# The order of the large products' matmuls: consecutive ones write different accumulators

## The chip, the core and the metric

The kernel runs on one core of one Trainium2 chip. The metric is the device time of one execution in microseconds, a median of three runs. TensorE (PE) multiplies, ScalarE (ACT) and VectorE (DVE) split the weights and evacuate the accumulators, SyncE (SP) starts the loads. Everything is computed in fp32 accuracy: each fp32 operand of a large product is split into a high and a low part of a matmul type ("hi" and "lo"), and hi·hi, hi·lo and lo·hi are summed.

## What is computed

Two transformer blocks run one after the other on 256 tokens of width 2048. What matters here are the products with weights; attention, convolution, pooling and norms lie between them.

```python
def first_block(x, ...):                      # two layers
    for l in range(DEPTH):
        h = _rms_norm(x, norm_g[l])
        proj = jnp.einsum('bsd,de->bse', h, w_in[l])           # 2048 -> 6208
        ...
        q_b = jnp.einsum('bsr,re->bse', _rms_norm(c_q, ...), w_uq[l])
        kv = jnp.einsum('bsr,re->bse', _rms_norm(c_kv, ...), w_ukv[l])
        ...
        x = x + jnp.einsum('bse,ed->bsd', mixed, w_out[l])     # 2048 -> 2048
    return _rms_norm(x, final_norm_g)

def second_block(x, mem, ...):                # one layer
    z = h @ w_in[l]                                            # 2048 -> 3584
    kv = m @ w_kv[l]
    ...
    x = x + mix @ w_out[l]
    u = causal_dwconv(h @ w_up[l], ffn_conv_w[l]) + ffn_conv_b[l]   # 2048 -> 11264
    gate, val = jnp.split(u, 2, axis=-1)
    x = x + (jax.nn.silu(gate) * val) @ w_down[l]              # 5632 -> 2048
    return rmsnorm(x, g_final)
```

## The kernel before

A large product takes 512 columns of a weight matrix at a time and sums over K in tiles of 128 rows ("k tiles"). `load_raw` (line 183) brings four k tiles of 512 columns in one transfer of 1 MB. `load_w` (line 188) splits them: ACT casts a k tile to `hi` (line 198), DVE subtracts and writes `lo` (line 199). Two k tiles make one hi tile and one lo tile; there are four buffers of each, so the split runs up to eight k tiles ahead of PE, and a cast into a buffer waits until PE has read the buffer's last user.

There are two kinds of product. `GemmA` gives tokens by columns: the activations are the stationary operand, the weights move. It has two accumulators, one for each half of the tokens, and three matmuls of up to 512 columns for each k tile and half (line 219). `GemmB` gives columns by tokens, in four blocks of 128 columns with one accumulator each: the weights are stationary and the activations move. For each k tile and block it has one matmul of 512 columns (hi weights times the hi and lo activations of all 256 tokens, line 244) and one of 256 columns (lo weights times hi activations, line 247).

One feed is two k tiles. Before, `GemmA.feed` goes through the halves in its outer loop, so six matmuls in a row write one accumulator; `GemmB.feed` goes through the blocks in its outer loop, so four in a row do.

The accumulators are PSUM banks. The pool `pg` (line 42) has four. A `GemmA` takes two of them, a `GemmB` all four, unless it is made with `alt=True`: then it takes the four banks of `pss`, `pst` and `pso`, which the attention and the transposes use as well. In the feed-forward part the products of the gate use `pg`, those of the value use the other four (lines 1040 and 1044). Elsewhere `GemmB` products follow one another, or are followed by a `GemmA`, in the same four banks of `pg`. A bank is free when its block has been evacuated: with a scale, ACT copies one half (line 256), DVE adds the other half out of PSUM (line 257) and multiplies (line 258). From line 257 on the next product may write the bank.

The products stand in the program one after another; `weave` puts pieces of attention between the feeds of a product. The order on each engine is then settled by a scheduler when the program is built, and each engine works through its instructions in that order.

Of the kernel before, what the change touches and what calls it, by code (L numbers as in the profile page):

```python
# [20 lines left out]
D = 2048  # L21
# [10 lines left out]
def net_kernel(ctx: ExitStack, tc: tile.TileContext, A: dict, out: bass.AP):  # L32
# [17 lines left out]
    def unit(shape, dt=F32, name="unit"):  # L50
        """A tile of 4 KiB per partition."""
        return units.tile(shape, dt, tag="u4", name=name)

# [1 line left out]
    xin = A["x"][0].rearrange("(t p) d -> p t d", p=128)  # L55
# [33 lines left out]
    cols = {}  # L89
# [28 lines left out]

# [1 line left out]
    def rsqrt(v, n, name):  # L120
# [47 lines left out]
    def bcast(col, name):  # L168
        """[128, 2] per-token column to [128, 256], the same on every partition."""
        dg = tp.tile([128, 2, 128], F32, tag="stage", name=f"{name}_d")  # L170
        for t in range(2):
            V.tensor_scalar(dg[:, t, :], ident, col[:, t:t + 1], None, ALU.mult)
        r = tp.tile([128, 256], F32, tag="R", name=name)

        def spread():
            p = pst.tile([128, 256], F32, tag="t", name=f"{name}_p")
            PE.matmul(p, ones, dg.rearrange("p t c -> p (t c)"), start=True, stop=True)
            V.tensor_copy(r, p)

        return r, spread  # L180

# [1 line left out]
    def load_raw(view, k0, nk, ncols):  # L183
# [19 lines left out]
    class GemmA:  # L203
        """out[tokens, cols], tokens in two tiles of 128; weights move."""

# [6 lines left out]
        def feed(self, items, act, tiles=(0, 1)):  # L212
            for t in tiles:
                for kt, hi, lo in items:
                    a = act(kt)
                    ah = a[:, 0, t * 128:(t + 1) * 128]
                    al = a[:, 1, t * 128:(t + 1) * 128]
                    for l, r in ((ah, hi), (al, hi), (ah, lo)):
                        PE.matmul(self.p[t][:, 0:self.w], l, r,  # L219
                                  start=self.c[t] == 0, stop=self.c[t] == self.n - 1)  # L220
                        self.c[t] += 1
# [4 lines left out]
    class GemmB:  # L226
        """out[cols, tokens] by blocks of 128 columns; tokens' hi and lo move."""

# [10 lines left out]
        def feed(self, items, act, bcols=None):  # L239
            for b in range(len(self.p)):  # L240
                for kt, hi, lo in items:
                    a = act(kt)
                    sl = slice(b * 128, (b + 1) * 128) if bcols is None else bcols(b)
                    PE.matmul(self.p[b], hi[:, sl], a.rearrange("p a t -> p (a t)"),  # L244
                              start=self.c[b] == 0, stop=False)
                    self.c[b] += 2
                    PE.matmul(self.p[b][:, 0:256], lo[:, sl], a[:, 0, :],  # L247
                              start=False, stop=self.c[b] == self.n)

# [10 lines left out]
    def gen(g, view, ncols, act, done=None, mid=()):  # L260
        """Feeds all of K; stops after each piece. mid: (first k after which, what to emit there)."""
        mid = dict(mid)
        for k0 in range(0, KT, 4):
            for it in load_w(view, k0, 4, ncols):
                g.feed(it, act)
                yield
            if k0 in mid:
                mid[k0]()
        if done:
            done(g)  # L270
# [6 lines left out]
    def weave(main, *fill, n=1):  # L277
        """One stage of main, then n pieces of fill, until both are through."""
        fill = itertools.chain(*fill)
        for _ in main:  # L280
            for _ in range(n):
                next(fill, None)
        run(fill)
# [11 lines left out]
    def lazy(make, *args, **kw):  # L295
        """A gen whose accumulators are taken when it starts."""
        yield from gen(make(), *args, **kw)
# [6 lines left out]
    def transpose_chunk(src, gcol, name):  # L304
        """src [128, 2, 512] token-major to [128, 4, hi/lo, 256] scaled by gcol[:, 0:4]."""
        dst = [unit([128, 2, 2, 256], F32R, f"{name}_{j}") for j in range(2)]
# [16 lines left out]

# [1 line left out]
    ssq = [cp.tile([128, 2, 4], F32, name=f"ssq{i}") for i in range(DEPTH + 3)]  # L325
# [36 lines left out]
    def setup_diff():  # L362
# [15 lines left out]

        # relative bias: r[h, i] for distance 255 - i, skewed through DRAM into T[p, h, c] = r[h, 127 - p + c]
        onehot = tp.tile([64, 384], F32, tag="pT", name="onehot", bufs=3)  # L380
# [76 lines left out]
    def bcast_row(row, name):  # L457
        """A row of D numbers on every partition."""
        ts_ = []
        for i in range(2):  # L460
            t = unit([128, 1024], F32, f"{name}{i}")
            SY.dma_start(t, row[i * 1024:(i + 1) * 1024].unsqueeze(0).to_broadcast([128, 1024]))
            ts_.append(t)
        return lambda n: ts_[n // 2][:, (n % 2) * 512:(n % 2 + 1) * 512]
# [25 lines left out]

# [1 line left out]
    rstd = keep(rstd0, 2, "rstd_0")  # L492
    HK = 0
    for l in range(DEPTH):
# [6 lines left out]

        # latent queries and keys, normalised and transposed; rotary key
        cT = []
# [34 lines left out]

        # second gate
        R, spread = bcast(rstd, f"R{l}")  # L540
# [81 lines left out]
        for i in range(2):  # L622
            SC.activation(sb[i], zb[i], AF.Silu)
        # latent attention, two heads at a time, among the products for the differential values
        M = [None] * 8
# [53 lines left out]

        # differential heads  # L680
        va = [unit([128, 2, 512], F32, f"va{i}") for i in range(2)]
# [79 lines left out]

        # output projection, residual, next hidden states
        wo = A["w_out"][l].rearrange("(k p) c -> p k c", p=128)
# [44 lines left out]

    # final norm of the first block, then the norm of the second one
    s2 = tp.tile([128, 2], F32, tag="ssq2", name="s2x")  # L810
# [6 lines left out]
    RX, spread = bcast(rx, "RX")  # L817
# [1 line left out]
    ivc = unit([128, 4, 256], F32, "ivc")  # L819
# [50 lines left out]
    def pool_out():  # L870
        yield
        yield
        # channels of group gi: even groups fill block b0 and the lower half of b1, odd ones the
        # upper half of b1 and block b2
        for blk in range(6):
# [18 lines left out]

    # queries and the attention over the memory
    g = runB(w[:, :, 3072:3584], 512, act, mid=[(HK, htail), (8, spread)])
# [44 lines left out]

    # pooling and convolution columns
    pol = [unit([128, 3, 256], F32, f"pooled{i}") for i in range(2)]
# [41 lines left out]

    # output projection and residual
    wo = A["w_out_2"][0].rearrange("(k p) c -> p k c", p=128)
# [29 lines left out]

# [1 line left out]
    act = tilesel(H)  # L1019
# [80 lines left out]
def _constants():  # L1100
    """Tables that depend on shapes alone."""
    f = np.float32
# [45 lines left out]
```

## Time and profile before

| | before |
|---|---|
| median of 3 runs | 1970.27 us (1970.2 to 1970.85) |
| span of the profiled execution | 1967.7 us |
| what lies around the span | 2.6 us |
| PE busy | 1952.5 us, 99% of the span |
| DVE busy | 1307.7 us, 66% |
| ACT busy | 1113.6 us, 57% |
| DMA | mean 191 GB/s |

The profile holds one execution, from its first instruction to its last: the span. The times of the runs are a little longer, as they hold the start and the end as well; the difference to the median is the third row. A matmul's row gives its start and its length; the length holds the time in which the result drains, which overlaps with the next matmul, so what one matmul costs is the distance from its start to the next start. Rows name tiles without their numbers: `gb` is any of a `GemmB`'s four accumulators in `pg`, `gbs`, `gbt` and `gbo` are those of a product with `alt=True`, `ga` is either half of a `GemmA`, `hf` the hidden states of the feed-forward part and `h` those of the layers.

### The profile page before, as it was taken

Reading aid. Unit: us, or ns where it says so; the run is one execution under the profiler, and the core shown is the slowest. Engines: PE = TensorE matmul, PEld = TensorE weight load, DVE = VectorE, ACT = ScalarE, POOL = GpSimd, SP = SyncE. Lnnn points to the kernel's source line nnn. Section 1 sums busy time; section 2 is a strip of 40 time slices with the busy share of each in tenths; the row PEclk is TensorE's granted clock in tenths of the full one; section 3 lists DMA queues with packets and bytes.
Section 4 is the critical chain, followed back from the end, with each engine's and each line's share of the span. In section 5 each row is a group of like instructions: output and inputs, shape, how many; then the busy total and the mean of one; then the engine's idle time right before and its main releaser. Section 6 shows DMA issues by size and latency. Waiting matters only on the chain.

```text
span 1967.7 us, 28785 instructions
## 1 busy us (share of the span) xinstructions
PE 1952.5 (99%) x10445; PEld 1665.0 (85%) x10445; DVE 1307.7 (66%) x2934; ACT 1113.6 (57%) x2403; POOL 10.1 (1%) x104
## 2 busy tenths in 40 slices
PE   8999999999999999999999999999999999999998
PEld 8988788888998788888887888888888888888887
DVE  6866556666576556766776676777786556777755
ACT  6755646665565555665554455665665445655544
POOL 0000000000000000000000000000000000000000
PEclk9999999999999999999999999999999999999999
DMA  8746455556665355456744566555556655555663
GB/s 253 274 161 195 153 177 166 172 171 227 197 202 183 122 168 167 158 193 222 250 151 153 180 229 231 176 195 207 193 177 209 225 203 182 176 190 202 217 222 129
DMA packets 190057, 376.66 MB, mean 191 GB/s; under 512 B 7495, under 2 KB 27994, under 8 KB 189786
## 3 DMA queue, kind: packets, MB, share of 16 engines
q1 hardware_dynamic: 189914, 374.82, 56.8%
q8 instruction: 82, 1.34, 0.3%
q14 instruction: 61, 0.50, 0.1%
HBM read 364.29 MB, written 12.07 MB: 191 GB/s over the span
## 4 chain that ended last, share of the span: by engine, by line
PE 98%; DVE 1%; ACT 1%; DMA 0%; issue 0%; ACTq 0%; SPq 0%; DVEq 0%
PE ga L219 40%; PE gb L244 23%; PE gb L247 12%; PE gbs L244 5%; PE gbs L247 2%; PE gbt L244 2%; PE gbo L244 2%; PE gbt L247 1%; PE gbo L247 1%; PE vb_ps L610 1%; PE s_b L640 1%; PE s_b L638 1%; PE s_a L708 1%; PE qr_ps L583 1%; PE pt L426 1%; PE pl_o L890 0%
## 5 line engine op out<-in xcount | busy, mean ns | idle before, releaser
L199 DVE TENSOR_TENSOR lo<-raw,hi 128x512 fp32r<-128x512 f32 (+4 forms) x1332 | 857.4, 679 | 532.6 <-ACT hi L198 527.6
L198 ACT CAST hi<-raw 128x512 fp32r<-128x512 f32 (+4 forms) x1332 | 756.3, 611 | 681.1 <-PE ga L219 260.9
L244 PE MATMUL gb<-h,hi 128*128 128x512 f32 x1088 | 389.0, 401 | 0.0
L247 PE MATMUL gb<-h,lo 128*128 128x256 f32 x1088 | 304.9, 280 | 0.0
L219 PE MATMUL ga<-hi,h 128*128 128x512 f32 (+2 forms) x896 | 261.0, 372 | 1.9 <-ACT hi L198 1.2
L244 PE MATMUL gb<-hf,hi 128*128 128x512 f32 x704 | 247.1, 396 | 0.0
L244 PEld LDWEIGHTS gb<-h,hi 128*128 128x128 f32 x1088 | 204.2, 188 | 49.5 <-issue 1.4
L219 PE MATMUL ga<-hi,gt 128*128 128x512 f32 (+1 forms) x784 | 221.0, 367 | 0.0
L247 PEld LDWEIGHTS gb<-h,lo 128*128 128x128 f32 x1088 | 205.3, 189 | 0.3
L247 PE MATMUL gb<-hf,lo 128*128 128x256 f32 x704 | 196.3, 279 | 0.0
L219 PEld LDWEIGHTS ga<-hi,h 128*128 128x128 f32 x896 | 160.7, 189 | 23.7 <-ACT hi L198 1.5
L219 PE MATMUL ga<-lo,h 128*128 128x512 f32 (+2 forms) x448 | 163.6, 366 | 0.0
L219 PEld LDWEIGHTS ga<-hi,gt 128*128 128x128 f32 x784 | 142.0, 189 | 24.4
L219 PE MATMUL ga<-hi,mix 128*128 128x512 f32 x512 | 161.1, 395 | 0.0
L244 PEld LDWEIGHTS gb<-hf,hi 128*128 128x128 f32 x704 | 132.1, 188 | 31.6
L219 PE MATMUL ga<-lo,gt 128*128 128x512 f32 (+1 forms) x392 | 144.0, 367 | 0.0
L247 PEld LDWEIGHTS gb<-hf,lo 128*128 128x128 f32 x704 | 132.6, 188 | 0.1
L244 PE MATMUL gbs<-hf,hi 128*128 128x512 f32 x352 | 127.1, 396 | 0.0
L219 PEld LDWEIGHTS ga<-hi,mix 128*128 128x128 f32 x512 | 94.5, 188 | 18.6
L219 PE MATMUL ga<-lo,mix 128*128 128x512 f32 x256 | 100.0, 391 | 0.0
L247 PE MATMUL gbs<-hf,lo 128*128 128x256 f32 x352 | 98.1, 279 | 0.0
L219 PEld LDWEIGHTS ga<-lo,h 128*128 128x128 f32 x448 | 84.3, 188 | 11.0
(336 smaller groups left out, 2575.2 us busy)
## 6 DMA issues: line engine op xcount, KB each, us to landing
raw<-in_w_in_dram SPq DMA_DIRECT2D x108, 1024.0 KB, 5.1
raw<-in_w_up_dram SPq DMA_DIRECT2D x88, 1024.0 KB, 4.9
raw<-in_w_out_dram SPq DMA_DIRECT2D x46, 1024.0 KB, 5.1
raw<-in_w_down_dram SPq DMA_DIRECT2D x39, 1024.0 KB, 5.2
raw<-in_w_in_dram SPq DMA_DIRECT2D x16, 704.0 KB, 4.3
raw<-in_w_kv_dram SPq DMA_DIRECT2D x8, 1024.0 KB, 5.3
raw<-in_w_ukv_dram SPq DMA_DIRECT2D x8, 1024.0 KB, 5.4
xdram<-x SPq DMA_DIRECT2D x16, 512.0 KB, 3.0
```

Of the source, the lines that this page charges most:

```text
L198: SC.copy(hi[:, i, :], raw[:, j + i, :])
L199: V.tensor_tensor(lo[:, i, :], raw[:, j + i, :], hi[:, i, :].bitcast(F32), ALU.subtract)
L219: PE.matmul(self.p[t][:, 0:self.w], l, r, start=self.c[t] == 0, stop=self.c[t] == self.n - 1)
L244: PE.matmul(self.p[b], hi[:, sl], a.rearrange("p a t -> p (a t)"), start=self.c[b] == 0, stop=False)
L247: PE.matmul(self.p[b][:, 0:256], lo[:, sl], a[:, 0, :], start=False, stop=self.c[b] == self.n)
L426: PE.transpose(pt[:, d:d + 128], e[:, j * 128:(j + 1) * 128], ident)
L583: PE.matmul(sp[:, t, 0:256], l_, r_.rearrange("p (h d) -> p h d", d=192)[:, :, 128:192], start=i == 0 and j == 0, stop=i == len(its) - 1 a ...
L610: PE.matmul(sp[:, t, :], l_, r_.rearrange("p (h d) -> p h d", d=256)[:, :, 128:256], start=n_[t] == 0, stop=n_[t] == 11)
L638: PE.matmul(s[:, a, c0:c1], qnT[hg][:, h % 4, q0:q0 + 128], knT[hg][:, h % 4, 0:kn], start=True, stop=False)
L640: PE.matmul(s[:, a, c0:c1], qrT[rs, hp, q0:q0 + 128], krT[rs, 0:kn], start=False, stop=True)
L708: PE.matmul(s[:, a, c0:c1], qa[rs, hh, q0:q0 + 128], ka[rs, hh, 0:kn], start=True, stop=True)
```

## The change

Both `feed` functions get another order of loops. In `GemmA` the halves are now the innermost loop: each of the three matmuls of a k tile is done for one half and then for the other. In `GemmB` the blocks are innermost: for each k tile first the four matmuls of 512 columns, one in each accumulator, then the four of 256 columns. The matmuls themselves, their operands, their number and the sums are the same. The changed lines stand at 217 (`ga`), 242 and 245 (`gb`) there. What else the diff holds are removed comments and docstrings, which move line numbers by two or three.

```diff
         def feed(self, items, act, tiles=(0, 1)):
-            for t in tiles:
-                for kt, hi, lo in items:
-                    a = act(kt)
-                    ah = a[:, 0, t * 128:(t + 1) * 128]
-                    al = a[:, 1, t * 128:(t + 1) * 128]
-                    for l, r in ((ah, hi), (al, hi), (ah, lo)):
-                        PE.matmul(self.p[t][:, 0:self.w], l, r,
+            for kt, hi, lo in items:
+                a = act(kt)
+                for h, r in ((0, hi), (1, hi), (0, lo)):
+                    for t in tiles:
+                        PE.matmul(self.p[t][:, 0:self.w], a[:, h, t * 128:(t + 1) * 128], r,
                                   start=self.c[t] == 0, stop=self.c[t] == self.n - 1)
                         self.c[t] += 1
...
         def feed(self, items, act, bcols=None):
-            for b in range(len(self.p)):
-                for kt, hi, lo in items:
-                    a = act(kt)
-                    sl = slice(b * 128, (b + 1) * 128) if bcols is None else bcols(b)
-                    PE.matmul(self.p[b], hi[:, sl], a.rearrange("p a t -> p (a t)"),
-                              start=self.c[b] == 0, stop=False)
+            for kt, hi, lo in items:
+                a = act(kt)
+                sl = [slice(b * 128, (b + 1) * 128) if bcols is None else bcols(b) for b in range(len(self.p))]
+                for b, p in enumerate(self.p):
+                    PE.matmul(p, hi[:, sl[b]], a.rearrange("p a t -> p (a t)"), start=self.c[b] == 0, stop=False)
                     self.c[b] += 2
-                    PE.matmul(self.p[b][:, 0:256], lo[:, sl], a[:, 0, :],
-                              start=False, stop=self.c[b] == self.n)
+                for b, p in enumerate(self.p):
+                    PE.matmul(p[:, 0:256], lo[:, sl[b]], a[:, 0, :], start=False, stop=self.c[b] == self.n)
```

How this stands on the engines is shown at one place, the end of the product for the first four query heads of the differential attention in the first layer (`gb0_2744` to `gb3_2747`, written to `qa0_2742`) and the start of the product for their keys (`gb0_2948` and on), which uses the same four banks. On PE, before, the last ten matmuls of the old product and the first two of the new one:

```order
L247 MATMUL gb1_2745<-h0_3_1_317,lo_2895 128x256
L244 MATMUL gb2_2746<-h0_3_1_317,hi_2894 128x512
L247 MATMUL gb2_2746<-h0_3_1_317,lo_2895 128x256
L244 MATMUL gb2_2746<-h0_3_1_317,hi_2894 128x512
L247 MATMUL gb2_2746<-h0_3_1_317,lo_2895 128x256
L244 MATMUL gb3_2747<-h0_3_1_317,hi_2894 128x512
L247 MATMUL gb3_2747<-h0_3_1_317,lo_2895 128x256
L244 MATMUL gb3_2747<-h0_3_1_317,hi_2894 128x512
L247 MATMUL gb3_2747<-h0_3_1_317,lo_2895 128x256
L244 MATMUL gb0_2948<-h0_0_0_118,hi_2954 128x512
L247 MATMUL gb0_2948<-h0_0_0_118,lo_2955 128x256
```

On PE now, the last eight of the old product and the first three of the new one:

```order
L242 MATMUL gb0_2744<-h0_3_1_317,hi_2894 128x512
L242 MATMUL gb1_2745<-h0_3_1_317,hi_2894 128x512
L242 MATMUL gb2_2746<-h0_3_1_317,hi_2894 128x512
L242 MATMUL gb3_2747<-h0_3_1_317,hi_2894 128x512
L245 MATMUL gb0_2744<-h0_3_1_317,lo_2895 128x256
L245 MATMUL gb1_2745<-h0_3_1_317,lo_2895 128x256
L245 MATMUL gb2_2746<-h0_3_1_317,lo_2895 128x256
L245 MATMUL gb3_2747<-h0_3_1_317,lo_2895 128x256
L242 MATMUL gb0_2948<-h0_0_0_118,hi_2954 128x512
L245 MATMUL gb0_2948<-h0_0_0_118,lo_2955 128x256
L242 MATMUL gb0_2948<-h0_0_0_118,hi_2954 128x512
```

The last matmul of the first accumulator stood twelve matmuls ahead of the old product's last one and stands three ahead of it now; the new product begins with that accumulator's bank, as before. On ACT the same place before (`hi_3006` is the hi tile of a later feed, in the buffer of `hi_2894`):

```order
L198 CAST hi_3000<-raw_2998 128x512 x2
L256 COPY ev_t_2932<-gb0_2744 128x256
L256 COPY ev_t_2936<-gb1_2745 128x256
L256 COPY ev_t_2940<-gb2_2746 128x256
L198 CAST hi_3006<-raw_2998 128x512
L256 COPY ev_t_2944<-gb3_2747 128x256
```

and now:

```order
L198 CAST hi_3000<-raw_2998 128x512 x2
L198 CAST hi_3006<-raw_2998 128x512
L253 COPY ev_t_2932<-gb0_2744 128x256
L253 COPY ev_t_2936<-gb1_2745 128x256
L253 COPY ev_t_2940<-gb2_2746 128x256
L253 COPY ev_t_2944<-gb3_2747 128x256
```

The first of the two casts to `hi_3006` has moved from behind the third evacuation to ahead of the first. On DVE the subtraction that belongs to it (`lo_3007`) has moved ahead of the additions; now it reads there:

```order
L199 TENSOR_TENSOR lo_3001<-raw_2998,hi_3000 128x512 x2
L199 TENSOR_TENSOR lo_3007<-raw_2998,hi_3006 128x512
L254 TENSOR_TENSOR ev_t_2932<-gb0_2744,ev_t_2932 128x256
L254 TENSOR_TENSOR ev_t_2936<-gb1_2745,ev_t_2936 128x256
L255 TENSOR_TENSOR qa0_2742<-ev_t_2932,R8_0_2212 128x256
```

Before, both halves of `lo_3007` stood behind all four evacuations.

## Rows read from the trace of the kernel before

**Rows 1.** The page: the span, the busy times of the engines with their number of instructions, and the chain that ended last by engine.

```profile
span 1967.7 us, 28785 instructions
...
PE 1952.5 (99%) x10445; PEld 1665.0 (85%) x10445; DVE 1307.7 (66%) x2934; ACT 1113.6 (57%) x2403; POOL 10.1 (1%) x104
...
PE 98%; DVE 1%; ACT 1%; DMA 0%; issue 0%; ACTq 0%; SPq 0%; DVEq 0%
```

**Rows 2.** Busy times in two stretches that cover nearly all of the span: start and end, length, busy us of each engine with its instructions, granted clock, DMA share, GB/s.

```profile
0.00:26.00 26.00, 20.36 (x107) 17.81 (x107) 15.66 (x47) 18.95 (x48) 0.38 (x7) 1.00 0.71 219
26.00:1960.00 1934.00, 1932.13 (x10338) 1647.23 (x10338) 1289.48 (x2878) 1093.34 (x2353) 9.71 (x97) 1.00 0.57 191
```

**Rows 3.** PE alone in order of time, in the output projection of the first layer, a `GemmA` with 512 columns: start us, length us, what, and how many in a row. The six matmuls from 476.23 write one half's accumulator, the six from 477.59 the other's, and from 478.95 it is the first one's again.

```profile
476.23 0.61 PE L219 MATMUL ga<-hi,mix 128*128 128x512 f32 x2
476.68 0.39 PE L219 MATMUL ga<-lo,mix 128*128 128x512 f32 x1
476.91 0.61 PE L219 MATMUL ga<-hi,mix 128*128 128x512 f32 x2
477.36 0.39 PE L219 MATMUL ga<-lo,mix 128*128 128x512 f32 x1
477.59 0.61 PE L219 MATMUL ga<-hi,mix 128*128 128x512 f32 x2
478.04 0.39 PE L219 MATMUL ga<-lo,mix 128*128 128x512 f32 x1
478.27 0.61 PE L219 MATMUL ga<-hi,mix 128*128 128x512 f32 x2
478.72 0.39 PE L219 MATMUL ga<-lo,mix 128*128 128x512 f32 x1
478.95 0.61 PE L219 MATMUL ga<-hi,mix 128*128 128x512 f32 x2
```

**Rows 4.** The same view near the end, in the only `GemmA` with 256 columns.

```profile
1935.00 0.40 PE L219 MATMUL ga<-hi,gt 128*128 128x256 f32 x2
1935.24 0.28 PE L219 MATMUL ga<-lo,gt 128*128 128x256 f32 x1
...
1936.08 0.40 PE L219 MATMUL ga<-hi,gt 128*128 128x256 f32 x2
```

**Rows 5.** The same view in the feed-forward part, a `GemmB`; eight pairs lie between the first and the last of these rows.

```profile
1301.30 0.39 PE L244 MATMUL gbt<-hf,hi 128*128 128x512 f32 x1
1301.53 0.27 PE L247 MATMUL gbt<-hf,lo 128*128 128x256 f32 x1
1301.64 0.40 PE L244 MATMUL gbt<-hf,hi 128*128 128x512 f32 x1
...
1304.07 0.39 PE L244 MATMUL gbt<-hf,hi 128*128 128x512 f32 x1
```

**Rows 6.** The same view at the place whose order is shown above: the last feed of the query product (eight pairs from 286.44) and the start of the key product at 289.27. The first accumulator's last matmul is the one at 287.04.

```profile
286.44 0.40 PE L244 MATMUL gb<-h,hi 128*128 128x512 f32 x1
286.68 0.28 PE L247 MATMUL gb<-h,lo 128*128 128x256 f32 x1
286.80 0.40 PE L244 MATMUL gb<-h,hi 128*128 128x512 f32 x1
287.04 0.28 PE L247 MATMUL gb<-h,lo 128*128 128x256 f32 x1
...
289.16 0.28 PE L247 MATMUL gb<-h,lo 128*128 128x256 f32 x1
289.27 0.40 PE L244 MATMUL gb<-h,hi 128*128 128x512 f32 x1
```

**Rows 7.** Two lines of the kernel with all their matmuls, by the tiles they read, the first and the last of each kind: count, then length in ns (least, median, greatest), first and last start. The eleven rows of line 244 hold 2,816 matmuls (704, 352, 176 and 176 of them read `hf`), line 247 as many; the ten of line 219 hold 3,768.

```profile
L244 PE MATMUL gb<-h,hi x1088: 389/395/582, 62.6 to 1111.1; 128*128 128x512 f32 x182
...
L244 PE MATMUL gbt<-h,hi x32: 392/394/395, 1068.4 to 1132.5; 128*128 128x512 f32 x32
```

```profile
L219 PE MATMUL ga<-hi,h x896: 318/389/690, 6.5 to 865.6; 128*128 128x512 f32 x103, 128*128 128x352 f32 x51, 128*128 128x384 f32 x26
...
L219 PE MATMUL ga<-lo,mixb x128: 387/389/397, 1134.0 to 1223.4; 128*128 128x512 f32 x128
```

**Rows 8.** ACT alone in order of time at the place of rows 6; in brackets the idle time ahead and what ended it.

```profile
286.52 1.14 ACT L198 CAST hi<-raw 128x512 fp32r<-128x512 f32 x2 [1.68 <-PE gb L244]
287.57 0.87 ACT L256 COPY ev_t<-gb 128x256 f32<-128x256 f32 x2
288.76 0.37 ACT L256 COPY ev_t<-gb 128x256 f32<-128x256 f32 x1 [0.32 <-PE gb L247]
289.36 0.62 ACT L198 CAST hi<-raw 128x512 fp32r<-128x512 f32 x1 [0.22 <-PE gb L244]
289.89 0.36 ACT L256 COPY ev_t<-gb 128x256 f32<-128x256 f32 x1
```

**Rows 9.** DVE alone at the same place.

```profile
287.18 1.29 DVE L199 TENSOR_TENSOR lo<-raw,hi 128x512 fp32r<-128x512 f32 x2 [1.53 <-ACT hi L198]
288.39 0.75 DVE L257 TENSOR_TENSOR ev_t<-gb,ev_t 128x256 f32<-128x256 f32 x2
```

**Rows 10.** All engines in order of time at a place where PE did wait for a bank: the fourth accumulator of a later query product, released by the addition on DVE.

```profile
343.35 0.42 DVE L257 TENSOR_TENSOR ev_t<-gb,ev_t 128x256 f32<-128x256 f32 x1
343.44 0.39 PE L435 MATMUL o_a<-va,pT 128*128 128x128 f32 x2
...
343.83 0.50 PE L244 MATMUL gb<-h,hi 128*128 128x512 f32 x1
...
344.16 0.28 PE L247 MATMUL gb<-h,lo 128*128 128x256 f32 x1
```

**Rows 11.** Who waited for whom: the waiting engine, tile and line, the one waited for, us in total, times, longest us.

```profile
ACT hi L198 <- PE ga L219: 260.9, 193, 4.0
...
ACT hi L198 <- PE gb L244: 194.3, 163, 2.5
```

## The prediction

> **What bounds the kernel now.** I read the page first: PE is busy for 99% of the span and makes 98% of the chain that ended last [rows 1]. Then the busy times by stretch: from 26 us on PE is busy for 1932.13 of 1934.00 us at a granted clock of 1.00, so it neither waits nor runs at the lower of its two clock levels [rows 2]. Only two things can therefore move the time: the step from one matmul's start to the next, and gaps in PE's work that are not there today. I read the steps from PE's own order of time in each kind of product, and the gaps from the three engines at one place where a product hands its accumulators to the next.
>
> **The step in the A products: no change.** In rows of 512 columns three matmuls take 0.68 us, 0.227 each [rows 3]. The accumulator changes between 477.36 and 477.59 and again between 478.72 and 478.95: 0.23 us both times, and the step from 476.68 to 476.91, where it does not change, is 0.23 as well. The 3,768 matmuls of line 219 [rows 7] already contain both cases at one price, so I cost the new order at 0. A row of 512 columns at 2.4 GHz streams for 0.213, so 0.013 us of each step is something else; the 256-column rows say the same (nine in 1.08 us, 0.120 each, against 0.107 of streaming [rows 4]).
>
> **The step in the B products: -6 us.** Here the trace has only alternating pairs of 512 and 256 columns. Eight pairs take 2.77 us in the feed-forward part, 0.346 a pair [rows 5], and 2.83 us, 0.354 a pair, at the query product [rows 6]. Four pairs, the work of one k tile, are 1.385 and 1.415. After the change a k tile is four matmuls of 512 and four of 256. By the nearest rows, those of the A products with equal neighbours, that is 3 x 0.227 + 3 x 0.120, and one alternating pair where the widths meet: 1.041 + 0.346 = 1.387, or 1.041 + 0.354 = 1.395. There are 2,816 pairs, 704 k tiles; half of the pairs read `hf` [rows 7]. So 352 x 0.002 = +1 and 352 x -0.020 = -7: I take -6. The bounds: every 512 as slow as the slowest here, 0.24 (286.44 to 286.68), gives 3 x 0.24 + 0.360 + 0.350 = 1.430 against a mean of 1.400, +21 us; every 256 as fast as 0.11 (1301.53 to 1301.64 [rows 5]) gives 0.681 + 0.330 + 0.350 = 1.361, -27 us. Both suppose that a step seen singly becomes the rule; I lean on the equal-neighbour rows and keep -12 to +8.
>
> The step of 0.120 is where I looked for a rule against the change: four matmuls of 256 columns in a row each need a new stationary operand of 128 columns. The Trainium skill, TensorE: Matmul & The Clock Gate, section LDWEIGHTS, gives such a load as columns over 1.2 GHz, 107 ns, as long as 256 columns stream, so by the page a run of 256s has nothing to spare, while in a pair the 512 has. The rows of the 256-column product agree with that (0.120 with a new operand each time), and the sum above already uses them; a load that took longer would cost 2,112 steps times the excess.
>
> **The gaps: +21 us.** This is the part that the loops don't show. A B product takes all four `pg` banks; a bank is free when DVE's addition (line 257) is through. Before, the first accumulator's last matmul starts at 287.04, 2.12 us ahead of the product's last one at 289.16 [rows 6]; its copy starts at 287.57 [rows 8], the first of two additions at 288.39, and half of the 0.75 later, at 288.77, the bank is free [rows 9]. PE asks for it at 289.27, half a microsecond later: no wait. From the last matmul's start to the free bank are 288.77 - 287.04 = 1.73 us. After the change the four accumulators end together: that matmul stands three ahead of the end, 3 x 0.120 = 0.36 us. With the old 1.73 the bank is free 1.37 us after the last matmul's start; PE could go on after 0.12. A gap of 1.25.
>
> The order adds to it. Ahead of the copies ACT now has a cast that waits for PE's last hi read; DVE has the subtraction of that cast ahead of the additions. Call T the start of the product's last matmul. The last 512 starts at T - 0.59 and its row is 0.40 long, so the cast starts at about T - 0.17. It takes 0.62 [rows 8], to T + 0.45; the copy starts within 0.53 of the cast (289.36 to 289.89) and is through at T + 0.73; the subtraction starts at T + 0.47, holds DVE for 0.60 (two and the first addition from 287.18 to 288.39 [rows 9]), so the addition runs from T + 1.07 to T + 1.47. Where PE did wait for a bank, its matmul started at 343.83, 0.06 after the addition's end at 343.77, and the next followed after 0.33 in place of 0.235, 0.10 more [rows 10]. So T + 1.53 against T + 0.12, and 0.10: **1.5 us** for one place.
>
> The places, from the code: query to key, key to second query, key to the second gate's A product, in two layers (6); memory keys to memory values (1); memory queries to the first columns, and the fifth to the first (2): 9 where nothing else stands between, 13.5 us. Seven have transposes, scores or values between, which PE can do meanwhile: the two gate products in each layer, the last gate to memory keys, second query to second key in each layer, sixth columns to fifth: half, 0.8 each, 5.5 us. The eight small products of w_uq and w_ukv have other matmuls beside them; 0.25 each, 2 us. The feed-forward part alternates two sets of banks and A products alternate pairs of banks: there the evacuation has a whole product's time, 0. The sum is 21; from 15 (the seven and the eight covered, 1.5 of slack lost) to 26 (all sixteen in full).
>
> **The sum.** 1967.7 + 21 - 6 = 1982.7 for the span; with the 2.6 that lie around it 1985.3, which compares to the median of 1970.27. I predict **1985 us**, 0.8% slower. Its own range is 1970.3 + 15 - 12 = 1973 to 1970.3 + 26 + 8 = 2004; I draw it a little closer, 1973 to 2000, as both ends at once are unlikely.
>
> **Rivals.**
> 1. The 0.013 us that each step has beyond streaming is the price of adding to the bank just written, and goes when neighbours write different banks. Over 3,768 + 5,632 matmuls that is 122 us, and with the gaps 1970 - 122 + 21 = 1869. Against it: the steps at which the accumulator changes cost the same to a hundredth [rows 3], in an A product and at every fourth matmul of a B product. 3%. The same skill page, section on the missing nanoseconds of a 56 ns step, puts back-to-back 512-column matmuls at 215.7 ns once warm, 11 ns below the 227 of this kernel; so by the page something here does cost extra, and that would be worth about 103 us if the order were its cause. The rows speak against that cause.
> 2. The B step gains more than I think, and the gaps are filled: the 512s behind one another fall to 0.227 and the 256s to 0.113 as the fast half of a pair in the query product does, 3 x 0.227 + 3 x 0.113 + 0.35 = 1.37 against 1.40, -21 us, and with only the nine bare places at 1.25 paid, +11: 1960. It decides for faster only if the gaps stay under 21. For it: casts wait for PE often (260.9 and 194.3 us [rows 11]), so the helpers are ahead. Against it: no row of 256 after 256 is below 0.12. 7%.
> 3. The gaps are hidden: the new product's operands have long been split, and if the additions ran ahead of the subtraction, only half the gap would be left at the bare places and none elsewhere, 9 x 0.7 = 6; with -6 from the step, 1970: no change. Against it: the order on ACT and DVE is fixed, and the cast and the subtraction stand ahead. 8%.
> 4. The evacuations, four at once in place of one every 0.7 us, starve the split. Then each of the 22 feed-forward products would lose about 1 us more: 2007. The casts' waits for PE [rows 11] say that the split is ahead by eight k tiles, 11 us; four evacuations take less. 6%.
>
> My forecast has 76%. Faster by over 0.2% (less than about 1966.3; 0.2% is what this kernel's runs can tell from nothing): rival 1, most of 2, 9%. Within 0.2%: rival 3 and the low tail, 10%. Slower: 81%.
>
> **What would show it.** The order of time at 289 us: PE idle for about 1.5 us with the addition on DVE as its releaser, and the same at the other eight bare places; PE's busy time nearly the same and the gaps listed under the B line's weight loads or matmuls as 15 to 25 us behind DVE's addition. The A steps stay at 0.227. In the feed-forward part no gap, and a k tile at 1.38 to 1.40. The prediction is wrong if A steps fall below 0.22, if 256 after 256 is not 0.120, or if PE goes on at a hand-over without a gap.

## The result: 1.25% slower, and the profile after

The changed kernel takes 1995.08 us (median of 4 runs, 1994.13 to 1995.5), the kernel before, on the same chip, 1970.56: the ratio is 1.0125, 95% interval 1.011 to 1.0139. Forecast were 1985 us. The page of the changed kernel, its lines of totals, its chain by engine, and two of its groups (line, engine, operation, count | busy us, mean ns of one | idle time just before them in us, and what ended it):

```profile
span 1993.7 us, 28835 instructions
...
PE 1960.8 (98%) x10445; PEld 1670.5 (84%) x10445; DVE 1303.6 (65%) x2934; ACT 1109.7 (56%) x2403; POOL 10.2 (1%) x104
...
PE 95%; DVE 2%; ACT 1%; DMA 1%; issue 0%; ACTq 0%; SPq 0%; DVEq 0%
...
L242 PE MATMUL gb<-h,hi 128*128 128x512 f32 x1088 | 309.8, 400 | 10.6 <-DVE ev_t L254 9.4
...
L242 PEld LDWEIGHTS gb<-h,hi 128*128 128x128 f32 x1088 | 185.5, 189 | 41.0 <-DVE ev_t L254 11.9
```

Against [rows 1] the span is 26.0 us longer. PE's idle time, span less busy time, goes from 15.2 to 32.9 us, +17.7; its busy time rises by 8.3. The other engines do the same work as before. On the chain PE falls by 3 points, and DVE and the DMAs stand one higher each: the end now hangs on other engines at times. The group names where: the first product line of the layers waits for line 254, DVE's addition that frees a bank. The list of who waited for whom says the same (us in total, times, longest us):

```profile
PEld gb L242 <- DVE ev_t L254: 13.0, 12, 1.5
...
PE gb L242 <- DVE ev_t L254: 9.8, 9, 1.3
...
PEld ga L217 <- DVE ev_t L254: 4.5, 3, 1.5
```

The loads (`PEld`) wait 13.0 us for it ahead of B products and 4.5 ahead of A products, 17.5 in all. The count of 9 in the second line is not that of the nine bare places: three of those stand ahead of an A product.

In the kernel before, the same wait is 0.4 us:

```profile
PEld gb L244 <- DVE ev_t L257: 0.4, 2, 0.2
```

Busy times by stretch, as in [rows 2], from 26 us to near the end:

```profile
26.00:1986.00 1960.00, 1940.30 (x10339) 1651.85 (x10338) 1285.84 (x2881) 1089.45 (x2353) 9.80 (x97) 1.00 0.57 188
```

The granted clock is 1.00 as before; PE lacks 19.7 us there where it lacked 1.9. So the loss is not the clock's: for most of it PE stands still.

One hand-over, the place of [rows 6, 8, 9]; the old product's last matmul now starts at 294.85 in place of 289.16. PE alone (start us, length us, what, how many in a row, in brackets the idle time ahead and what ended it):

```profile
292.16 1.09 PE L242 MATMUL gb<-h,hi 128*128 128x512 f32 x4
293.09 0.64 PE L245 MATMUL gb<-h,lo 128*128 128x256 f32 x4
293.57 1.09 PE L242 MATMUL gb<-h,hi 128*128 128x512 f32 x4
294.50 0.63 PE L245 MATMUL gb<-h,lo 128*128 128x256 f32 x4
296.43 0.50 PE L242 MATMUL gb<-h,hi 128*128 128x512 f32 x1 [1.30 <-DVE ev_t L254]
296.77 0.28 PE L245 MATMUL gb<-h,lo 128*128 128x256 f32 x1
```

ACT and then DVE at the same place:

```profile
294.70 0.62 ACT L198 CAST hi<-raw 128x512 fp32r<-128x512 f32 x1 [1.66 <-PE gb L242]
295.22 1.19 ACT L253 COPY ev_t<-gb 128x256 f32<-128x256 f32 x4
296.28 0.65 ACT L198 CAST hi<-raw 128x512 fp32r<-128x512 f32 x1
```

```profile
295.35 0.69 DVE L199 TENSOR_TENSOR lo<-raw,hi 128x512 fp32r<-128x512 f32 x1 [1.51 <-ACT hi L198]
295.96 0.74 DVE L254 TENSOR_TENSOR ev_t<-gb,ev_t 128x256 f32<-128x256 f32 x2
296.63 0.75 DVE L255 TENSOR_TENSOR qa<-ev_t,R 128x256 f32<-128x256 f32 x2
```

The old product's last matmul is the fourth from 294.50, three steps of 0.118 later: T = 294.85. The reader can follow the prediction's chain with it: cast at T - 0.15 (forecast -0.17), subtraction at T + 0.50 (0.47), addition at T + 1.11 (1.07) and 0.41 long, so through at T + 1.52 (1.47), PE at T + 1.58 (1.53), the next matmul 0.34 after it (0.33). Without the wait PE would have gone on at T + 0.12: 1.46 us are lost, and the late next matmul costs 0.10 more. All nine places that the prediction called bare show the wait, each between 1.45 and 1.46 us.

The steps, read from starts. An A product (six matmuls from 500.44 to 501.80, 0.227 each, as in [rows 3]) and a B product of the feed-forward part:

```profile
500.44 0.62 PE L217 MATMUL ga<-lo,mix 128*128 128x512 f32 x2
500.90 1.07 PE L217 MATMUL ga<-hi,mix 128*128 128x512 f32 x4
501.80 0.62 PE L217 MATMUL ga<-lo,mix 128*128 128x512 f32 x2
```

```profile
1298.42 1.09 PE L242 MATMUL gb<-hf,hi 128*128 128x512 f32 x4
1299.35 0.64 PE L245 MATMUL gb<-hf,lo 128*128 128x256 f32 x4
1299.83 1.09 PE L242 MATMUL gb<-hf,hi 128*128 128x512 f32 x4
1300.76 0.63 PE L245 MATMUL gb<-hf,lo 128*128 128x256 f32 x4
1301.23 1.09 PE L242 MATMUL gb<-hf,hi 128*128 128x512 f32 x4
```

A k tile of the B product takes 1.41 and 1.40 us here, against 1.385 in [rows 5]. Split by neighbours over the first group of feed-forward products, 512 after 512 steps by 0.2335 us on average, 512 to 256 by 0.2286, 256 to 256 by 0.1186, 256 to 512 by 0.1183; 3 x 0.2335 + 0.2286 + 3 x 0.1186 + 0.1183 = 1.403. No product of this part has a gap.

### The profile page after: what moved, and what is told of

It is laid out like the page before. It is cut to its first block, busy times and chain, and to the rows that moved or that the text cites. A ratio compares the mean times of both kernels' runs of the same rounds, so it can differ in the third digit from the quotient of the medians.

```text
span 1993.7 us, 28835 instructions
## 1 busy us (share of the span) xinstructions
PE 1960.8 (98%) x10445; PEld 1670.5 (84%) x10445; DVE 1303.6 (65%) x2934; ACT 1109.7 (56%) x2403; POOL 10.2 (1%) x104
## 4 chain that ended last, share of the span: by engine, by line
PE 95%; DVE 2%; ACT 1%; DMA 1%; issue 0%; ACTq 0%; SPq 0%; DVEq 0%
PE ga L217 38%; PE gb L242 23%; PE gb L245 11%; PE gbs L242 5%; PE gbs L245 2%; PE gbt L242 2%; PE gbo L242 2%; PE gbo L245 1%; PE gbt L245 1%; PE vb_ps L607 1%; DVE lo L199 1%; PE s_b L637 1%; PE s_b L635 1%; DMA raw<-in_w_in_dram 1%; ACT hi L198 1%; PE s_a L705 1%
## 5 line engine op out<-in xcount | busy, mean ns | idle before, releaser
L242 PE MATMUL gb<-h,hi 128*128 128x512 f32 x1088 | 309.8, 400 | 10.6 <-DVE ev_t L254 9.4
L217 PE MATMUL ga<-hi,h 128*128 128x512 f32 (+2 forms) x896 | 226.1, 373 | 4.7 <-DVE ev_t L254 2.6
L217 PE MATMUL ga<-hi,gt 128*128 128x512 f32 (+1 forms) x784 | 193.5, 367 | 0.0
L242 PE MATMUL gb<-hf,hi 128*128 128x512 f32 x704 | 193.0, 395 | 0.0
L245 PEld LDWEIGHTS gb<-h,lo 128*128 128x128 f32 x1088 | 169.9, 188 | 23.6
L245 PE MATMUL gb<-h,lo 128*128 128x256 f32 x1088 | 180.6, 281 | 0.0
L217 PE MATMUL ga<-lo,h 128*128 128x512 f32 (+2 forms) x448 | 127.6, 365 | 0.0
L217 PE MATMUL ga<-lo,gt 128*128 128x512 f32 (+1 forms) x392 | 114.1, 367 | 0.0
L245 PE MATMUL gb<-hf,lo 128*128 128x256 f32 x704 | 112.6, 281 | 0.0
L217 PEld LDWEIGHTS ga<-lo,gt 128*128 128x128 f32 x392 | 71.9, 189 | 12.2
```

Of the source, the lines that this page charges most:

```text
L217: PE.matmul(self.p[t][:, 0:self.w], a[:, h, t * 128:(t + 1) * 128], r, start=self.c[t] == 0, stop=self.c[t] == self.n - 1)
L242: PE.matmul(p, hi[:, sl[b]], a.rearrange("p a t -> p (a t)"), start=self.c[b] == 0, stop=False)
L245: PE.matmul(p[:, 0:256], lo[:, sl[b]], a[:, 0, :], start=False, stop=self.c[b] == self.n)
```

## The experiments

The theory to be tried (hand-over): rotating through the accumulators lets all four end together, their evacuation can no longer run beside the product's tail, and PE waits at each product that takes the same banks. Its rival (pace): the steps themselves became longer.

**The two halves of the change apart.** `e1_only_a` has the new order in `GemmA` alone, `e2_only_b` in `GemmB` alone (each a part of the diff above).

> Only the A products get the new order; the B products keep the old one. Theory 'hand-over' (the 24.5 us come from the four accumulators of a B product ending together, so that PE waits for a bank at the next product): A products alternate pairs of banks and no B product ends differently, so 1970 to 1971, the A steps at 0.227 us and no gap over 0.5 us after 30 us. Rival 'pace' (writing another accumulator at each step costs something everywhere): about a third of the loss, 1977 to 1980. My sum had 0 for this part.

Measured: 1971.93 us, ratio 1.0006 (0.9997 to 1.0015). The new order of the A products cannot be told from none.

> Only the B products get the new order; the A products keep the old one. Hand-over: the whole loss, 1993 to 1996, with nine gaps of about 1.45 us behind DVE's addition. Pace: two thirds of the loss, 1985 to 1988.

Measured: 1994.2 us, ratio 1.0119 (1.0104 to 1.0134). The loss is in the B products.

**Gaps or steps.** Two kernels exchange the order of one piece, the last two k tiles of each B product, against that of the rest. `e3_last_by_block` is the changed kernel with the last piece in the old order:

```diff
+            if self.c[0] + 2 * len(items) == self.n:
+                for b in range(len(self.p)):
+                    for kt, hi, lo in items:
+                        (the two matmuls of before)
+            else:
                 for kt, hi, lo in items:
                     (the eight matmuls of after)
```

`e4_last_rotating` is the kernel before with the last piece alone in the new order.

> As the changed kernel, but the last feed of each B product goes block by block as before, so that the four accumulators end one after another; 7 of 8 feeds keep the new order. Hand-over: the nine gaps vanish and 20 us or more come back, 1970 to 1974; what is left over 1970 is the price of the new steps. Pace: seven eighths of the loss stay, 1991 to 1993. A third theory, 'supply' (four evacuations at once delay the split of the weights): the evacuations are spread again here, so it expects 1970 to 1974 too, and differs from hand-over only in what PE waits for: hi and lo in place of the addition.

Measured: 1975.62 us, ratio 1.0025 (1.0016 to 1.0035). 19.5 us are back.

> The mirror of it: the kernel before, in which only the last feed of each B product rotates through the accumulators. Hand-over: nearly the whole loss, 1990 to 1994, with the same nine gaps. Pace: one eighth of the loss in the B products, 1972 to 1974.

Measured: 1988.87 us, ratio 1.0092 (1.0075 to 1.0108): 18.1 of the 24.5 us come with one piece of each product in the new order. Both kernels land on the hand-over's side of the two theories, and neither inside its range: the first is 1.6 us above, the second 1.1 below. PE at the same hand-over, first in `e3_last_by_block`, then in `e4_last_rotating`:

```profile
291.55 0.39 PE L243 MATMUL gb<-h,hi 128*128 128x512 f32 x1
291.78 0.28 PE L246 MATMUL gb<-h,lo 128*128 128x256 f32 x1
291.89 0.63 PE L253 MATMUL gb<-h,hi 128*128 128x512 f32 x2
```

```profile
292.13 0.63 PE L248 MATMUL gb<-h,lo 128*128 128x256 f32 x4
294.06 0.50 PE L254 MATMUL gb<-h,hi 128*128 128x512 f32 x1 [1.30 <-DVE ev_t L267]
```

In the first, the new product starts 0.11 us after the old one's last matmul; in the second, the 1.30 us of idle time behind DVE's addition are there in a kernel whose products are otherwise those of before.

Where the spans part is read from the first matmul of each product, in one kernel and in another. Changed kernel less `e3_last_by_block`, that is the order of the last piece alone: 3.0 us up to the first differential product of the first layer, 5.3 in that layer's four differential products, 1.5 and 5.2 in the second layer, 4.0 in the second block up to the feed-forward part, 0.7 from there: 19.7 in all. `e3_last_by_block` less `e1_only_a`, the rotating order without its end: 3.2 us before the feed-forward part and 0.9 in it (12 products of the first group each longer by 0.23, 10 of the second shorter by 0.19), 4.2 in all. `e1_only_a` less the kernel before: 2.1, of which 1.0 is there at 62 us, before any B product; the profiled span of before, 1967.7, is 0.3 us below its lowest on the chips of the experiments, so part of the 2.1 is the spread of the runs; the medians differ by 1.15. The sum is 26.0.

Of the 3.0 us, 1.0 arises at 64 us, before any B product has ended, and so not from the last piece. There PE waits in the first gate for 1.32 us, until ACT has copied the A product before it out of the bank (line 524); ACT came to it late, as casts ahead of the copy had waited for the DMA. `e6_key_alt` below has the same program up to there and does not wait. The changed kernel and then `e6_key_alt`:

```profile
65.81 0.50 PE L242 MATMUL gb<-h,hi 128*128 128x512 f32 x1 [1.16 <-ACT kr L524]
```

```profile
64.28 0.63 PE L242 MATMUL gb<-h,hi 128*128 128x512 f32 x2
```

In `e3_last_by_block` the same wait is 0.3 us, and two traces of one kernel (`e5_pairs` and `e11_pairs_again` below) have none and 0.3. So the last piece accounts for about 18.7 us of the span, and the steps for about 3.9.

**Other ways to take the gap away.** `e6_key_alt` is the changed kernel with the first key product of each layer in the other set of four banks (`alt=True`), so that two hand-overs in each layer no longer meet the same banks.

> The changed kernel with the first key product of each layer in the other four banks (those of the attention), nothing else. Hand-over: the gaps from first query to first key and from first key to second query go, two in each layer, 4 x 1.45 = 5.8 us: 1988 to 1990. Pace or supply: no change, 1995.

Measured: 1988.9 us, ratio 1.0093 (1.0078 to 1.0108), 6.2 us less than the changed kernel; four gaps of 1.455 are 5.8. The gaps at the four hand-overs are gone from its trace.

`e7_act_frees_bank` is the changed kernel with ACT copying the whole bank, so that the bank is free without DVE's addition:

```diff
-                SC.copy(t[:, 256:512], self.p[b][:, 256:512])
-                V.tensor_tensor(t[:, 0:256], self.p[b][:, 0:256], t[:, 256:512], ALU.add)
+                SC.copy(t, self.p[b])
+                V.tensor_tensor(t[:, 0:256], t[:, 0:256], t[:, 256:512], ALU.add)
```

> The changed kernel, but a scaled evacuation copies all 512 columns on ACT and DVE adds from SBUF, so that the bank is free after ACT's copy and does not wait for DVE, which has the subtraction ahead of the addition. Hand-over, with the working of the prediction: the copy starts at T + 0.36 and takes 0.59, PE goes on at about T + 1.0 in place of T + 1.5, so each of the nine gaps falls from 1.45 to 0.7 or 0.9 and the time to 1985 to 1990. If the subtraction ahead of the addition did not matter, the longer copy would leave the gap or lengthen it: 1994 to 1997.

Measured: 1987.68 us, ratio 1.0086 (1.0069 to 1.0103). PE at the hand-over:

```profile
293.90 0.63 PE L245 MATMUL gb<-h,lo 128*128 128x256 f32 x4
295.25 0.50 PE L242 MATMUL gb<-h,hi 128*128 128x512 f32 x1 [0.72 <-ACT ev_t L253]
```

The releaser is now ACT's copy, and the nine gaps are 0.88 us each in place of 1.455, 5.2 us of the 7.4 that it gains. The length of the wait is that of the evacuation's chain; that is the hand-over's mechanism in its size. How much of it comes from the cast and the subtraction that stand ahead of the evacuation, no run separates. An estimate from the rows of the changed kernel: the first accumulator's last matmul (start 294.50, 0.28 long) is through at T - 0.07; a copy of 0.38 and an addition of 0.41 right behind it would let PE go on at about T + 0.8, a wait of 0.7 in place of 1.46.

**The order that keeps blocks together at the end, and still changes accumulators.** `e5_pairs` has, in all but the last piece, the k tile outside and the blocks inside, each block with its 512- and its 256-column matmul side by side: every second matmul goes to another accumulator, and the widths alternate as before. The last piece is by blocks.

> As the kernel with the last feed block by block, but in the other feeds each k tile takes the blocks in turn with a pair of 512 and 256 columns for each, so the accumulator changes after every pair and the widths alternate as before. Theory 'the accumulator does not matter, only which widths follow each other' : B pairs at 0.346 to 0.354 us as before, 1970 to 1972. If changing the accumulator did cost or give something in the B products, the pair's step would differ from the old 0.350 by more than 0.002 (over 2 us per 1000 pairs, 6 us in all).

Measured: 1973.33 us, ratio 1.0008 (0.9999 to 1.0017), but its ten runs lie in two groups, four at 1968.63 to 1969.47 and six at 1972.72 to 1974.62; runs of before spread by 1.5 us. The profiled run is of the lower group, and so is that of a repetition, `e11_pairs_again`, 1968.6 us:

> The kernel with pairs again, for a second trace: its times lay at 1969 and at 1974 us. Should this run be one of 1974 us, the trace tells where the 5 us lie: with two paces of the pairs, 0.346 and 0.354 us, all of it in one or both groups of the feed-forward products (0.42 us a product, 22 products: 4 to 9 us); with a gap that comes and goes, at one or two places and no change of pace. Should it be one of 1969 us, nothing new.

So where the 5 us lie was not seen. How the lower group makes up for what it loses is seen: up to the end of the first group of feed-forward products the profiled run is 4.1 us behind the kernel before, and in the second group nine of ten products are 0.42 us shorter and the first 0.28, so that nothing is left. A second group at the longer pace would add these 4.1 us, most of the 5; no trace of such a run was kept. At the same time, before (four pairs in 1.41 us from 1700.29) and then `e5_pairs` (1.38 from 1700.28):

```profile
1700.29 0.40 PE L244 MATMUL gbo<-hf,hi 128*128 128x512 f32 x1
...
1701.70 0.40 PE L244 MATMUL gbs<-hf,hi 128*128 128x512 f32 x1
```

```profile
1700.28 0.39 PE L253 MATMUL gbt<-hf,hi 128*128 128x512 f32 x1
...
1701.66 0.39 PE L253 MATMUL gbt<-hf,hi 128*128 128x512 f32 x1
```

The same two widths in turn, over a product at 0.353 and at 0.347 us a pair (22.61 and 22.19 us for its 64 pairs). The two paces of the prediction [rows 5, 6] are thus not two kinds of product: before, the first group of feed-forward products runs at the shorter and the second, the same code, at the longer.

**What sets the step.** Three more orders, all with blocks ending one after the other. `e8_hi_first` is `e3_last_by_block` with all eight 512-column matmuls of a piece ahead of its eight of 256; `e9_block_hi_hi_lo_lo` is the kernel before with, in each block's piece, 512, 512, 256, 256 in place of 512, 256, 512, 256; `e10_last_hi_hi_lo_lo` is the same in the last piece alone:

```diff
+            acts = [act(kt) for kt, _, _ in items]
             for b, p in enumerate(self.p):
+                for (kt, hi, lo), a in zip(items, acts):
+                    (512 columns, hi)
+                for (kt, hi, lo), a in zip(items, acts):
+                    (256 columns, lo)
```

> The kernel with the last piece by blocks (1975.6 us), but within each earlier piece of two k tiles all eight 512-column matmuls come first, each block in turn, and then all eight 256-column ones. By the hand-over theory no 1.45 us gap: as 1975.6 but for the steps. For the steps, theory S1: the 512-column step of the rotating order is 0.233 us and not 0.227 because 512- and 256-column matmuls alternate in groups of four; in longer groups it comes nearer to the 0.227 of the token products, and the time falls by 0.003 to 0.006 us times about 2,600 steps, to 1960 to 1968 us. Theory S2: 0.233 belongs to these products' 512-column matmuls whatever stands beside them: 1974 to 1977 us.

Measured: 1972.87 us, ratio 1.0013 (1.0004 to 1.0022), in neither range. One group of eight, with the first of 256 behind it:

```profile
1300.89 0.63 PE L253 MATMUL gbs<-hf,hi 128*128 128x512 f32 x2
1301.36 0.39 PE L253 MATMUL gbt<-hf,hi 128*128 128x512 f32 x1
1301.59 0.40 PE L253 MATMUL gbo<-hf,hi 128*128 128x512 f32 x1
1301.82 0.62 PE L253 MATMUL gbs<-hf,hi 128*128 128x512 f32 x2
1302.28 0.39 PE L253 MATMUL gbt<-hf,hi 128*128 128x512 f32 x1
1302.50 0.39 PE L253 MATMUL gbo<-hf,hi 128*128 128x512 f32 x1
1302.73 0.40 PE L258 MATMUL gbs<-hf,lo 128*128 128x256 f32 x2
```

Read to the nanosecond, the eight steps are, as medians over the feed-forward part, 0.233, 0.236, 0.228, 0.232, 0.231, 0.227, 0.227 and, to the first of 256, 0.227 us. The mechanism of S1 is there, but it takes five steps behind the 256s until the 0.227 of the A products is reached, so the mean of 512 after 512 falls from 0.2335 to 0.2303 only.

> The kernel before, but within one block's two k tiles of a piece the two 512-column matmuls come first and then the two 256-column ones; blocks one after the other as before, so no gap at the hand-overs. Theory S1 (steps follow the mix of sizes): two like sizes beside each other take 0.228 + 0.2285 + 0.118 + 0.119 = 0.693 us for two pairs, 0.347 a pair, where before has 0.346 in one part and 0.354 in another: 1966 to 1969 us. Theory S3 (two paces, and which one a stretch falls into is not set by the order within a block): 1970 to 1972 us, with a stretch of 0.354 left.

Measured: 1966.4 us, ratio 0.9979 (0.997 to 0.9988): faster than the kernel before by 0.2%, inside the range of S1. In order of time:

```profile
1300.46 0.63 PE L244 MATMUL gbo<-hf,hi 128*128 128x512 f32 x2
1300.93 0.40 PE L247 MATMUL gbo<-hf,lo 128*128 128x256 f32 x2
1301.16 0.63 PE L244 MATMUL gbs<-hf,hi 128*128 128x512 f32 x2
1301.63 0.39 PE L247 MATMUL gbs<-hf,lo 128*128 128x256 f32 x2
1301.86 0.62 PE L244 MATMUL gbs<-hf,hi 128*128 128x512 f32 x2
```

Two pairs take 0.70 us; over a whole group 0.348 a pair in both groups, where before has 0.347 and 0.353, so no stretch of 0.353 is left, against S3. The second down projection starts 3.8 us earlier than before: 3.2 are ten products of the second group at 0.32 each, 0.6 stem from ahead of them.

> The kernel before, but in the last piece of each block product alone the two 512-column matmuls of a block come first and then its two 256-column ones. No gap at the hand-overs by the hand-over theory. Theory S3 (a break in the series of pairs at the end of each product lets the next product begin at the shorter of two paces, as the kernel with a rotating last piece seems to show with 0.39 us less for each of the last ten products): 1965 to 1968 us. Otherwise 1970 to 1971.5 us.

Measured: 1967.63 us, ratio 0.9985 (0.9976 to 0.9994). The time is in the range of S3. The first, second, third and fourth of the last ten products begin at:

```profile
1623.10 0.39 PE L255 MATMUL gb<-hf,hi 128*128 128x512 f32 x1
...
1645.67 0.40 PE L255 MATMUL gbs<-hf,hi 128*128 128x512 f32 x1
...
1668.25 0.40 PE L255 MATMUL gb<-hf,hi 128*128 128x512 f32 x1
...
1690.45 0.40 PE L255 MATMUL gbs<-hf,hi 128*128 128x512 f32 x1
```

The first two still take 22.57 and 22.58 us, 0.353 a pair; the other eight take 22.20, 0.41 less than before, 0.347 a pair. So the shorter pace follows breaks of the series at a product's end, but not in the next product: it came with the third. `e4_last_rotating` has the same two and eight, so the 0.39 that the expectation gives to each of its last ten products holds for eight.

## Why the prediction was right in direction and short in size

Its main step holds. The bare hand-over was put at 1.5 us, 1.41 of it the wait and 0.10 the late next matmul; the wait is 1.45 to 1.46, in each of the nine places, and the 0.10 are there as well; every instant of the chain from the cast to PE's restart lies within 0.05 us of the working. That DVE's addition would be the releaser, that no gap would come in the feed-forward part, that ACT's cast and DVE's subtraction stand ahead of the evacuation: all as read from the rows. The total of this step, forecast 21 us, is 19.7 by the last-piece exchange (span), 18.7 without the wait at 64 us, and 18.1 to 19.5 by the medians. The nine waits make 13.1 of it. The seven half-covered places and the eight small products, forecast 7.5, make the rest before the feed-forward part: 19.0 less 13.1 and the 1.0 at 64 us, 4.9. The small products give next to nothing, 0.4 us or less in each layer.

The A step, forecast 0, holds within the measurement: 0.227 us after as before, and +1.15 us by the medians. A small part of the hand-over shows here too: both halves of an A product now end together, and the transposes behind the latent products start 0.62 us after the product's last matmul at 57 us and 0.63 at 564, where it was 0.32.

**The step that failed is "The step in the B products: -6 us".** It measured +4.2 us in the span, 3.9 without the wait at 64 us, and +3.7 by the medians (1975.62 less 1970.78, less the 1.15 of the A half). By the medians the forecast was 9.5 us short: this term 9.7, the A half 1.15, and against them the hand-overs, 1.5 too dear. It took 512 after 512 from the A products, 0.227, because the neighbours are equal there; in a B product it is 0.2335, since three 512s behind four 256s never get to the price of a long run, as `e8_hi_first` shows step by step. 256 after 256, taken as 0.120 from a series with only 256s, is 0.1186, which gives back a little. A k tile thus takes 1.403 us where the forecast had 1.391 in the mean; over 704 k tiles that is 8.4 of the 9.7. The mean before, forecast 1.400, came out about right by luck (1.399 in the feed-forward products): rows 5 (0.346) stood for all feed-forward products and rows 6 (0.354) for all others, but the second group of the former runs at 0.353, and others that nothing interrupts, as those from 583 and 1089 us, at 0.347 (22.07 us from first to last matmul, against 22.49 in the one from 266.7). The rows of before did show the warning: within a pair the 512 takes 0.23 to 0.24 beside a 256 [rows 5, 6]. The bounds, -12 to +8, held it. Of the prediction's signs two did not come as written: PE's busy time rose by 8.3 us, and a k tile takes 1.40 to 1.41 us, where 1.38 to 1.40 was named.

The 2.6 us around the span were 1.8 here (1995.5 of the profiled execution less 1993.7), and 1.7 to 1.9 in the runs of the experiments. By these the profiled execution before, with its span of 1967.7, stands for a time of about 1969.5 us, below the median that the 2.6 was taken from.

The rivals. The first (each step loses 0.013 us because it adds to the bank just written) falls: A's accumulators alternate in every step and nothing changes, 1.0006 (0.9997 to 1.0015). The Trainium skill, TensorE: Matmul & The Clock Gate, in the section on the missing nanoseconds of a 56 ns step, has back-to-back 512-column matmuls at 215.7 ns; long runs of 512s settle at 226 to 227 ns here whichever accumulators they write, so what lies between is not their order. The second (steps gain more than gaps cost) falls by the measured +4. The third (gaps hidden) falls by the nine waits: operands were split in time, but the bank was not free. The fourth (the split starves, 1 us for each feed-forward product) falls: these products change by +0.26 us in the first group and by -0.16 in the second, without gaps.

Open stays why one series of pairs runs at 0.347 or 0.353 us, why a 512-column step depends on the matmuls before it, and where the 5 us between the two groups of runs of `e5_pairs` lie.

## What to carry to other kernels

An order of matmuls also sets when each accumulator is finished: with accumulators taken in turn they all finish at once, and a product that needs the same banks waits for a whole evacuation, here 1.46 us at each of nine hand-overs, with what ACT and DVE do ahead of it. Finish them one after another at least in the last piece of a product, or give the next product other banks. A step is to be priced from rows with the same sequence of widths, not with equal neighbours alone.

## What the runs showed of the hardware that was not expected

- Changing the accumulator from one matmul to the next is worth nothing measurable: 0.227 us (median) a step of 512 columns either way, in the 2,952 matmuls of that width in the A products.
- A 512-column step depends on what ran several matmuls earlier: 0.233, 0.236, 0.228, 0.232, 0.231 and only then 0.227 us behind a group of eight 256s (medians of the feed-forward part of `e8_hi_first`).
- A series of alternating 512 and 256 columns has two paces, 0.347 and 0.353 us a pair, and keeps the one it has through ten products (4 us here); with two like widths behind each other at each product's end the shorter one came back, from the third product on.
- Every 256-column step of the B products, least 0.112 us, is above the 107 ns that come, as an estimate, out of the Trainium skill, TensorE: Matmul & The Clock Gate, section LDWEIGHTS (columns over 1.2 GHz) for loading a 128-column stationary operand. The rows of these loads are 188 to 189 ns long and overlap the matmuls, so their length does not show what one load costs, and no run here shows that this load is what binds the steps.
